# Two RWKV head pairs in step, on 64x64 products, in a hybrid mLSTM and RWKV-7 layer

## The chip, the cores and the metric

One core of a Trainium2 chip runs the whole layer for one sequence of 2048 tokens, width 1024. The metric is the time of one execution on the device in microseconds (us). TensorE's clock has two levels, 1.2 and 2.4 GHz; the profile gives the granted clock as a share of the higher one.

## The reference, cut to what matters

The layer normalises its input, projects it (`u @ w_in`), and feeds two groups of heads. Four mLSTM heads of 128 use a convolution, a gated matrix memory and an output gate. Eight RWKV-7 heads of 64 use a recurrence over tokens:

```python
def step(S, inp):
    r_t, w_t, k_t, v_t, a_t, b_t = inp
    sa = jnp.einsum('bhij,bhj->bhi', S, a_t)
    S = S * w_t[:, :, None, :] + sa[..., None] * b_t[:, :, None, :] + v_t[..., None] * k_t[:, :, None, :]
    return S, jnp.einsum('bhij,bhj->bhi', S, r_t)
```

`S` is a 64x64 state per head. The outputs of a head are normalised over its 64 values (mean and variance), scaled, given a bonus `sum(r*k*r_k)*v`, and gated. An output projection, cross-attention into 256 memory tokens, and a SwiGLU feed-forward part follow; the change touches none of these.

## The kernel before, in words

The first stage (`pre_pass`) normalises and transposes the input into f16 high and low halves, kept in device memory as `u_d`. The mixer then makes four passes (`mixer_pass`, `hp`), one for each pair of RWKV heads (128 columns: a head on each 64 partitions) and one mLSTM head. A pass loads and splits its own weights (`wraw`, L262 to L266, then `split`, L48 and L49), then goes through eight blocks of 256 tokens. Large products (`mm3`, L53 to L55) are three f16 products each, high times high, high times low, low times high.

RWKV is computed in chunks of 64 tokens, four to a block. `prepare` makes, for a block, the three projections `kps`, `rps`, `vps`, the decays, and the operands AR (read side) and KB (write side). It turns `v` (L368) and KB (L391) by TensorE's transpose, and multiplies KB by AR (`aps`, L379), where each head uses its own 64 rows but 128 columns of weights. The products are masked (L383 to L386) into M, RR and AY. `solve` inverts the triangular matrices of two blocks together, on GpSimd in 31 steps (L420, L422) with trips through device memory. `scan` carries the state through the four chunks: R from L458, times the inverse (L467), and the new state from L472, with the old state and the values stacked on all 128 rows: a head's state stands on its own 64 rows and its values on the other head's. ScalarE copies each result out of PSUM (L460, L470), VectorE decays and adds (L464, L476). When the last chunk is through, the outputs `yps` (L482, L485) are computed. A `tail` normalises them, later.

Blocks go in groups of two: prepare both, solve both, scan them one after the other, then the mLSTM part of both. The `u` pool holds eight tiles of each half, that is two blocks. A planner orders the instructions on each engine before the run, from its own estimate of their times; each engine then executes its queue in that order. In the last pass the mLSTM parts of the last four blocks are put behind everything else.

Of the kernel before, what the change touches and what calls it, by code (L numbers as in the profile page):

```python
# [105 lines left out]
def rwkv_consts(c, pool, I):  # L106
# [10 lines left out]
    c.ind = pool.tile([P, 2], F32, name="ind")  # L117
    nc.vector.memset(c.ind, 0.0)
    nc.vector.memset(c.ind[0:64, 0:1], 1.0)
    nc.vector.memset(c.ind[64:128, 1:2], 1.0)  # L120
# [124 lines left out]
def mixer_pass(c, I, hp, tp, T):  # L245
# [3 lines left out]
    GS = min(2, T // SGN)  # L249
    w_in = I["w_in"][0]  # L250
    ct = hp
    cs = slice(ct * P, (ct + 1) * P)
# [3 lines left out]
    cols = [Q0 + ct * P, Q0 + 512 + ct * P, Q0 + 1024 + ct * P, ct * P, 512 + ct * P, 1024 + ct * P, 1536 + ct * P]  # L256
    wts = [], []
    for n, o in ((3, Q0), (4, 0)):
        for k in range(KT):
            wk = w_in[k * P:(k + 1) * P, :]  # L260
            raw = tp.x.tile([P, n * P], F32, tag=f"wraw{n}", name="wraw", bufs=4 if n == 3 else 2)
            nc.sync.dma_start(raw.rearrange("p (j c) -> p j c", j=n),  # L262
                              wk[:, o:o + 512 * n].rearrange("p (j c) -> p j c", j=n)[:, :, cs])
            h = tp.w.tile([P, n * P], F16, tag=f"wh{n}", name="wh", bufs=12 if n == 3 else 9)
            l = tp.w.tile([P, n * P], F16, tag=f"wl{n}", name="wl", bufs=12 if n == 3 else 9)
            split(nc, h, l, raw, c.gmix[:, k:k + 1])  # L266
            wts[n - 3].append((h, l))

    carry = tp.k.tile([P, 3], F32, tag="carry", name="carry")
    nc.gpsimd.memset(carry, 0.0)  # L270
    Sc = tp.k.tile([P, 64], F32, tag="Sc", name="Sc")
    nc.gpsimd.memset(Sc, 0.0)
    halo = tp.k.tile([P, 2, 3], F32, tag="halo", name="halo")
    nc.gpsimd.memset(halo, 0.0)
    st = Ctx()
    st.Cn = tp.m2.tile([P, P + 1], F32, tag="Cn", name="Cn")
    nc.gpsimd.memset(st.Cn, 0.0)

    def project(ps, j, u):
        for k in range(KT):  # L280
            h, l = wts[j > 2][k]
            o = (j - 3 if j > 2 else j) * P
            s = slice(o, o + P)
            mm3(nc, ps, (h[:, s], l[:, s]), u[k], k == 0, k == KT - 1)

    def shifted(ps, j, o):
        t = tp.t2.tile([P, SGN + 1], F32, tag="tmu", name="tmu")
        m = 4 * j + ct
        nc.gpsimd.tensor_copy(t[:, 0:1], carry[:, j:j + 1])
        nc.scalar.activation(t[:, 1:SGN + 1], ps, AF.Copy, scale=c.mu_s[:, m:m + 1])  # L290
        nc.gpsimd.tensor_copy(carry[:, j:j + 1], t[:, SGN:SGN + 1])
        nc.vector.scalar_tensor_tensor(o, ps, c.mu_c[:, m:m + 1], t[:, 0:SGN], op0=ALU.mult, op1=ALU.add)  # L292
        return o

    def prepare(sg, u, M):
        g = Ctx()
        t0 = sg * SGN
        xwa = [tp.t2.tile([P, SGN], F16, tag=f"xwa{i}", name="xwa") for i in range(2)]
        for i in range(2):
            nc.sync.dma_start(xwa[i], c.l_d[0][i][:, t0:t0 + SGN])  # L300
        sl = tp.sl
        AR = tp.t1.tile([P, 4, P], F32, tag="AR", name="AR")
        g.RR = next(tp.RR)
        g.M = M
        g.AY = sl.tile([P, 4, 2, 64], F32, tag="AY", name="AY")
        g.KBt = sl.tile([P, 4, 2, 64], F32, tag="KBt", name="KBt")
        g.VS = sl.tile([P, 4, 2, 64], F32, tag="VS", name="VS")
        g.VX = sl.tile([P, 4, 2, 64], F32, tag="VX", name="VX")
        g.bon = sl.tile([P, SGN], F32, tag="bon", name="bon")
        g.W = sl.tile([P, 4, 1], F32, tag="W", name="W")  # L310
        KB = tp.t1.tile([P, 4, 192], F32, tag="KB", name="KB")
# [19 lines left out]
        nc.gpsimd.tensor_copy(g.W, E[:, :, 64:65])  # L331

        ps = tp.pmm.tile([P, SGN], F32, tag="mm", name="kps")
        project(ps, 1, u)
        k = shifted(ps, 1, tp.t2.tile([P, SGN], F32, tag="k", name="k"))
        ps = tp.pmm.tile([P, SGN], F32, tag="mm", name="rps")
        project(ps, 0, u)
        r = shifted(ps, 0, tp.t2.tile([P, SGN], F32, tag="r", name="r"))
        ps = tp.pmm.tile([P, SGN], F32, tag="mm", name="vps")
        project(ps, 2, u)  # L340
        v = shifted(ps, 2, tp.t2.tile([P, SGN], F32, tag="v", name="v"))
# [18 lines left out]
        nc.scalar.copy(KB[:, :, 128:192], KB[:, :, 0:64])  # L360
# [4 lines left out]
        nc.vector.tensor_tensor(g.bon, bps, v, ALU.mult)  # L365
        vps = tp.pax.tile([P, 2, P], F32, tag="ax", name="vps")
        for m in range(2):
            nc.tensor.transpose(vps[:, m], v[:, m * P:(m + 1) * P], c.ident)  # L368
        for h in range(2):
            for e in range(2):  # L370
                nc.scalar.copy(g.VS[halves[1 - h], e::2, h], vps[halves[e], :, 64 * h:64 * h + 64])
        for h in range(2):
            nc.gpsimd.tensor_copy(g.VX[halves[1 - h], :, h], g.VS[halves[1 - h], :, h])
        kcs = [slice(64 * (1 - h), 64 * (1 - h) + P) for h in range(2)]
        axs = [tp.pax.tile([P, 4, P], F32, tag="ax", name="aps") for _ in range(2)]
        for n in range(4):
            for h in range(2):
                b = halves[h]
                nc.tensor.matmul(axs[h][:, n], lhsT=KB[b, n, kcs[h]], rhs=AR[b, n], start=True, stop=True)  # L379
        for h in range(2):  # L380
            b, ob, aps = halves[h], halves[1 - h], axs[h]
            bc = lambda r, cc: c.mask[r, cc].unsqueeze(1).to_broadcast([r.stop - r.start, 4, 64])
            nc.vector.tensor_tensor(g.M[b], aps[b, :, 0:64], bc(b, b0), ALU.mult)  # L383
            nc.vector.tensor_tensor(g.RR[ob, :, h, 0:64], aps[ob, :, 0:64], bc(ob, b0), ALU.mult)
            nc.scalar.copy(g.RR[b, :, h], AR[b])
            nc.vector.tensor_tensor(g.AY[:, :, h], aps[:, :, 64:128], bc(slice(0, P), b1), ALU.mult)  # L386
        kps = [tp.pax.tile([P, 4, 64], F32, tag="ax", name="kbps") for _ in range(2)]
        for n in range(4):
            for h in range(2):
                b = halves[h]  # L390
                nc.tensor.transpose(kps[h][:, n], KB[b, n, kcs[h]], c.ident[b, b])  # L391
        for h in range(2):
            nc.scalar.copy(g.KBt[:, :, h], kps[h])
        return g

    def solve(MX, NG):
# [3 lines left out]
        MXu = MX.rearrange("p g u t -> p (g u) t")  # L400
# [49 lines left out]
    def scan(sg, g, g2, fresh):  # L450
        y = tp.s2.tile([P, 2, 2, 64], F32, tag="y", name="y")
        if fresh:
            for h in range(2):
                nc.scalar.copy(g.VS[halves[h], 0, h], Sc[halves[h]])
        for n in range(4):
            ch = tp.psc.tile([P, 3, 64], F32, tag="ch", name="ch")
            for h in range(2):
                nc.tensor.matmul(ch[halves[h], 0], lhsT=g.RR[:, n, h, 0:64], rhs=g.VS[:, n, h], start=True, stop=True)  # L458
            R = tp.s2.tile([P, 64], F32, tag="R", name="R")
            nc.scalar.copy(R, ch[:, 0])  # L460
            Sw = tp.s2.tile([P, 64], F32, tag="Sw", name="Sw")
            for h in range(2):
                b = halves[h]
                nc.vector.tensor_scalar(Sw[b], g.VS[b, n, h], g.W[b, n], None, op0=ALU.mult)  # L464
            for h in range(2):
                b = halves[h]
                nc.tensor.matmul(ch[b, 1], lhsT=g.M[b, n], rhs=R[b], start=True, stop=True)  # L467
            for h in range(2):
                b = halves[h]
                nc.scalar.copy(g.VX[b, n, h], ch[b, 1])  # L470
            for h in range(2):
                last = nc.tensor.matmul(ch[halves[h], 2], lhsT=g.KBt[:, n, h], rhs=g.VX[:, n, h], start=True, stop=True)  # L472
            for h in range(2):
                b = halves[h]
                dst = g.VS[b, n + 1, h] if n < 3 else g2.VS[b, 0, h] if g2 is not None else Sc[b]
                nc.vector.scalar_tensor_tensor(dst, ch[b, 2], g.W[b, n], Sw[b], op0=ALU.mult, op1=ALU.add)  # L476
        yps = tp.psc.tile([P, 2, 2, 64], F32, tag="Y", name="yps")
        with tc.issue_after(last.ins):
            for m in range(2):
                for h in range(2):  # L480
                    for n in (2 * m, 2 * m + 1):
                        nc.tensor.matmul(yps[halves[n % 2], m, h], lhsT=g.RR[:, n, h, 64:128], rhs=g.VS[:, n, h],  # L482
                                         start=True, stop=False)
                    for n in (2 * m, 2 * m + 1):
                        nc.tensor.matmul(yps[halves[n % 2], m, h], lhsT=g.AY[:, n, h], rhs=g.VX[:, n, h],  # L485
                                         start=False, stop=True)
        nc.vector.tensor_copy(y, yps)

        def tail():
            y4 = y.rearrange("p m h i -> p (m h) i")  # L490
            mean = tp.s2.tile([P, 4], F32, tag="mean", name="mean")
# [930 lines left out]
```

## Time and profile before

| what | us |
|---|---|
| median of three runs | 3099.39 |
| the runs | 3096.95, 3099.39, 3101.4 |
| profiled execution | 3100.74 |
| its span, first to last instruction | 3099.0 |

A matmul's time in the trace runs from its start to the modelled end of its result, so matmuls overlap: how fast they follow one another is read from their starts. PE is TensorE's products, PEld its weight loads, DVE is VectorE, ACT is ScalarE, POOL is GpSimd. A shape such as 64*64 64x64 f32 gives the rows and columns of the array that the weights take, then the shape of what streams through. An entry in brackets behind a row tells how long the engine was idle before it and what ended that. The page puts the feed-forward part and the attention behind the mixer; the profile rows that follow are of the mixer and of its start.

### The profile page before, as it was taken

The numbers are of one execution on the slowest core, as the hardware profiler recorded it, in microseconds if no ns is written. First come the engines' busy times: TensorE is split into PE (matmuls) and PEld (weight loads), VectorE is DVE, ScalarE is ACT, GpSimd is POOL, SyncE is SP. The second block draws the span as 40 slices with busy tenths as digits, with TensorE's granted clock in tenths as the row PEclk, the third lists the DMA queues.
The fourth block names the chain that finished last, engine by engine and source line by source line (L and its number), as shares of the span: only waits on it lengthen the run. The fifth ranks groups of instructions, "written<-read, shape, count | busy, mean of one in ns | idle before, by whom it ended". The sixth has DMA issues, their size and how long they took to land. (4 is left out here: it accounts for less than half of the span.)

```text
span 3099.0 us, 55710 instructions
## 1 busy us (share of the span) xinstructions
PE 2956.4 (95%) x20515; PEld 1776.2 (57%) x20515; DVE 2155.9 (70%) x4150; ACT 1299.8 (42%) x3098; POOL 1199.7 (39%) x2189
## 2 busy tenths in 40 slices
PE   7799999999999988999999999999999999899998
PEld 4577777778777767646555554444444444344443
DVE  6568877787687867627788887554454555897975
ACT  6445544554455445506656654222222222423332
POOL 2156654555555665003412134222222221644642
PEclk9899999999999988999999999999999999999999
DMA  8522422232232223555323357122111111554442
GB/s 278 130 76 63 105 70 68 76 97 75 63 80 64 77 70 99 183 167 171 124 76 108 107 194 242 58 67 67 55 55 55 55 58 58 184 185 145 151 144 75
DMA packets 393966, 331.01 MB, mean 107 GB/s; under 512 B 92654, under 2 KB 343772, under 8 KB 392796
## 3 DMA queue, kind: packets, MB, share of 16 engines
q1 hardware_dynamic: 393692, 327.45, 34.5%
q8 instruction: 161, 2.64, 0.3%
q14 instruction: 113, 0.93, 0.1%
HBM read 231.86 MB, written 95.49 MB: 106 GB/s over the span
## 5 line engine op out<-in xcount | busy, mean ns | idle before, releaser
L53 PE MATMUL pp<-u,wb 128*128 128x512 f16 x1232 | 467.5, 379 | 13.5 <-DVE e L1127 10.1
L54 PE MATMUL pp<-u,wb 128*128 128x512 f16 x1232 | 467.7, 380 | 0.0
L55 PE MATMUL pp<-u,wb 128*128 128x512 f16 x1232 | 467.3, 380 | 0.0
L1127 DVE TENSOR_TENSOR e<-pp,e 128x512 f32<-128x512 f32 x308 | 208.5, 689 | 301.6 <-PE pp L55 288.1
L55 PE MATMUL dps<-w,gS 128*128 128x512 f16 x616 | 234.6, 381 | 7.5 <-DVE gS L49 7.5
L54 PE MATMUL dps<-w,gS 128*128 128x512 f16 x616 | 234.7, 381 | 1.7 <-DVE w L49 1.7
L53 PE MATMUL dps<-w,gS 128*128 128x512 f16 x616 | 234.8, 381 | 0.0
L420 POOL TENSOR_TENSOR tmp<-M,X 64x126 f32<-64x126 f32 (+22 forms) x496 | 194.9, 393 | 74.2 <-DMA M<-md 45.9
L422 POOL TENSOR_TENSOR X<-X,tmp 64x126 f32<-64x126 f32 (+22 forms) x496 | 204.3, 412 | 30.1
L54 PEld LDWEIGHTS <-wb 128*128 128x128 f16 x1232 | 120.6, 98 | 157.1 <-issue 13.4
L53 PEld LDWEIGHTS <-wb 128*128 128x128 f16 x1232 | 120.7, 98 | 149.5 <-DMA u<-u_d 3.9
L55 PEld LDWEIGHTS <-wb 128*128 128x128 f16 x1232 | 120.7, 98 | 146.0 <-issue 0.6
L1143 POOL TENSOR_TENSOR S<-raw 128x512 f32<-128x512 f32 x22 | 33.3, 1515 | 411.2 <-DVE wb L49 411.2
L54 PEld LDWEIGHTS <-wh 128*128 128x128 f16 x1280 | 128.0, 100 | 36.0 <-issue 16.1
L53 PE MATMUL qps<-uh,wh 128*128 128x256 f16 x512 | 140.8, 275 | 2.0 <-DVE r L292 1.1
L53 PEld LDWEIGHTS <-wh 128*128 128x128 f16 x1280 | 128.4, 100 | 24.3 <-issue 2.2
L55 PEld LDWEIGHTS <-wl 128*128 128x128 f16 x1280 | 128.3, 100 | 22.5 <-issue 1.9
L53 PE MATMUL vops<-wh,uh 128*128 128x256 f16 x512 | 139.9, 273 | 1.1 <-ACT cv L539 0.8
L55 PE MATMUL qps<-uh,wl 128*128 128x256 f16 x512 | 140.6, 275 | 0.0
L54 PE MATMUL qps<-ul,wh 128*128 128x256 f16 x512 | 140.5, 274 | 0.0
L55 PE MATMUL vops<-wh,ul 128*128 128x256 f16 x512 | 139.8, 273 | 0.0
L54 PE MATMUL vops<-wl,uh 128*128 128x256 f16 x512 | 139.7, 273 | 0.0
(428 smaller groups left out, 7895.2 us busy)
## 6 DMA issues: line engine op xcount, KB each, us to landing
g_d<-e SPq DMA_DIRECT2D x88, 256.0 KB
uh<-u_d SPq DMA_DIRECT2D x144, 128.0 KB
ul<-u_d SPq DMA_DIRECT2D x144, 128.0 KB
h<-h_d SPq DMA_DIRECT2D x32, 512.0 KB
acc<-h_d SPq DMA_DIRECT2D x32, 512.0 KB
u_d<-ub SPq DMA_DIRECT2D x56, 256.0 KB
ga<-g_d SPq DMA_DIRECT2D x32, 384.0 KB
raw<-in_ffn_w_gate_dram SPq DMA_DIRECT2D x22, 512.0 KB
```

The costliest lines, as they stand in the source:

```text
L53: nc.tensor.matmul(out, lhsT=lhs[0], rhs=rhs[0], start=start, stop=False)
L54: nc.tensor.matmul(out, lhsT=lhs[0], rhs=rhs[1], start=False, stop=False)
L55: nc.tensor.matmul(out, lhsT=lhs[1], rhs=rhs[0], start=False, stop=stop)
L420: nc.gpsimd.tensor_tensor(tv, M[:, s, s + 1:32].unsqueeze(2).to_broadcast(shp), X[:, s, 0:ncl].unsqueeze(1).to_broadcast(shp), ALU.mult)
L422: nc.gpsimd.tensor_tensor(X[:, s + 1:32, 0:ncl], X[:, s + 1:32, 0:ncl], tv, ALU.add)
L1127: add = lambda o, x, y: nc.vector.tensor_tensor(o, x, y, ALU.add)
L1143: nc.gpsimd.tensor_tensor(s[0], a[1][0], a[1][1], ALU.add)
```

## The change

Two passes (`hq`) take the place of four. A pass loads the weights of two head pairs and two mLSTM heads, in eight tiles of each kind (raw tiles: two and one buffers, before four and two). A group is now one block with both pairs (`e` is 0 or 1): prepare both, solve both together, scan both in step, then the two mLSTM parts.

All small RWKV products now use a head's own 64 rows and its own 64 columns. The values V and what was VX (now X) are no longer stacked with the other head's state; each of the chain's and of the outputs' products gets one part for each operand. Transposes of v, KB and y become products with the identity (`turn`); v's uses `cent`, the identity minus 1/64, so that the values have zero mean over a head and the tail's mean is not computed. The state's decay is applied in one instruction for both pairs, after an addition for both. The bonus keeps the values as they were.

```diff
-            raw = tp.x.tile([P, n * P], F32, tag=f"wraw{n}", name="wraw", bufs=4 if n == 3 else 2)
-            h = tp.w.tile([P, n * P], F16, tag=f"wh{n}", name="wh", bufs=12 if n == 3 else 9)
+            raw = tp.x.tile([P, n * 2 * P], F32, tag=f"wraw{n}", name="wraw", bufs=2 if n == 3 else 1)
+            h = tp.w.tile([P, n * 2 * P], F16, tag=f"wh{n}", name="wh", bufs=8)
...
+    c.cent = pool.tile([P, 64], F32, name="cent")
+    for b in (0, 64):
+        nc.vector.tensor_scalar(c.cent[b:b + 64], c.ident[b:b + 64, b:b + 64], -1.0 / 64, None, op0=ALU.add)
...
+    def turn(out, x, by):
+        nc.tensor.matmul(out, lhsT=x, rhs=by, start=True, stop=True)
...
-            nc.tensor.transpose(vps[:, m], v[:, m * P:(m + 1) * P], c.ident)
+                turn(vps[halves[h], n], v[halves[h], n * 64:n * 64 + 64], c.cent[halves[h]])
+        nc.scalar.copy(G.V[:, e], vps)
+        for o, dst in ((64, g.M), (0, g.KY)):
+            aps = tp.pax.tile([P, 4, P], F32, tag="ax", name="aps")
+            for n in range(4):
+                for h in range(2):
+                    b = halves[h]
+                    nc.tensor.matmul(aps[b, n], lhsT=KB[b, n, o:o + 64], rhs=AR[b, n], start=True, stop=True)
+            nc.vector.tensor_tensor(dst, aps, c.mask.unsqueeze(1).to_broadcast([P, 4, P]), ALU.mult)
...
+                    turn(kps[halves[h], n, i], KB[halves[h], n, 64 * i:64 * i + 64], c.ident[halves[h], halves[h]])
...
+        def both(out, *parts):
+            for i, (l, r) in enumerate(parts):
+                for b in halves:
+                    last = nc.tensor.matmul(out[b], lhsT=l[b], rhs=r[b], start=i == 0, stop=i == len(parts) - 1)
+            return last
         for n in range(4):
+            S = state(n)
+            ch = tp.psc.tile([P, 2, 3, 64], F32, tag="ch", name="ch")
+            for e, g in enumerate(gs):
+                both(ch[:, e, 0], (g.AR[:, n, 0:64], S[:, e]), (g.KY[:, n, 0:64], G.V[:, e, n]))
+            R = tp.s2.tile([P, 2, 64], F32, tag="R", name="R")
+            nc.scalar.copy(R, ch[:, :, 0])
+            for e, g in enumerate(gs):
+                both(ch[:, e, 1], (g.M[:, n, 0:64], R[:, e]))
+            nc.scalar.copy(G.X[:, :, n], ch[:, :, 1])
+            for e, g in enumerate(gs):
+                last = both(ch[:, e, 2], (g.KBt[:, n, 1], G.X[:, e, n]), (g.KBt[:, n, 0], G.V[:, e, n]))
+            Sn = tp.s2.tile([P, 2, 64], F32, tag="Sn", name="Sn")
+            nc.vector.tensor_tensor(Sn, ch[:, :, 2], S, ALU.add)
...
+            nc.vector.tensor_tensor(dst, Sn, G.W[:, :, n].to_broadcast([P, 2, 64]), ALU.mult)
...
+                    both(yps[:, e, n], (g.AR[:, n, 64:128], state(n)[:, e]), (g.M[:, n, 64:128], G.X[:, e, n]),
+                         (g.KY[:, n, 64:128], G.V[:, e, n]))
...
+                        turn(tps[b, e, n * 64:n * 64 + 64], y[b, e, n], c.ident[b, b])
...
+    for sg in range(NS):
+        u = load_u(sg)
+        G = group(sg)
+        gs = [prepare(sg, e, u, G) for e in range(2)]
+        solve(G.MX, 2)
+        stails.append(scan(sg, gs, G))
```

## Rows read from the trace of the kernel before

**Rows 1.** The page, part 1: engine, busy us (share of the span) xinstructions.

```profile
PE 2956.4 (95%) x20515; PEld 1776.2 (57%) x20515; DVE 2155.9 (70%) x4150; ACT 1299.8 (42%) x3098; POOL 1199.7 (39%) x2189
```

**Rows 2.** Windows view: start:end, length, engines' busy time, clock, DMA share, GB/s.

```profile
130.00:1215.00 1085.00, 1021.18 (x10297) 812.10 (x10298) 818.17 (x2110) 533.45 (x1631) 596.14 (x1599) 0.96 0.29 75
```

**Rows 3.** Timeline of TensorE, one chain burst: start, us, line, shape, count.

```profile
686.56 0.27 PE L55 MATMUL qps<-uh,wl 128*128 128x256 f16 x1
686.67 0.27 PE L53 MATMUL qps<-uh,wh 128*128 128x256 f16 x1
686.87 0.33 PE L467 MATMUL ch<-R,MX 64*64 64x64 f32 x4
687.14 0.28 PE L54 MATMUL qps<-ul,wh 128*128 128x256 f16 x1
```

**Rows 4.** The timeline of TensorE in an output burst (yps).

```profile
733.24 0.34 PE L472 MATMUL ch<-VX,KBt 128*64 128x64 f32 x4
733.41 0.29 PE L482 MATMUL yps<-VS,RR 128*64 128x64 f32 x4
733.52 0.29 PE L485 MATMUL yps<-VX,AY 128*64 128x64 f32 x4
733.64 0.29 PE L482 MATMUL yps<-VS,RR 128*64 128x64 f32 x4
```

**Rows 5.** Lines view, TensorE, shapes apart: count, busy us, mean ns, idle before.

```profile
L458 PE MATMUL ch<-VS,RR 128*64 128x64 f32 x512 | 47.4, 254 | 13.6 <-DVE VS L476 9.3 <-DVE Sc L476 2.9 <-ACT VS L454 1.0
L391 PE MATMUL kbps<-ident,KB 64*128 64x64 f32 x256 | 28.6, 244 | 1.4 <-DVE AY L386 0.9 <-ACT KBt L393 0.2
```

**Rows 6.** The timeline of TensorE around one aps burst.

```profile
631.87 0.27 PE L53 MATMUL kps<-uh,wh 128*128 128x256 f16 x1
632.08 1.16 PE L379 MATMUL aps<-AR,KB 64*128 64x128 f32 x8
633.16 0.28 PE L54 MATMUL kps<-ul,wh 128*128 128x256 f16 x1
```

**Rows 7.** The timeline of TensorE around kbps and vps transposes.

```profile
690.48 0.38 PE L368 MATMUL vps<-ident,v 128*128 128x128 f32 x2
690.70 0.27 PE L55 MATMUL qps<-uh,wl 128*128 128x256 f16 x1
...
747.41 0.27 PE L55 MATMUL gps<-xg,lg 128*128 128x256 f16 x1
747.61 0.46 PE L391 MATMUL kbps<-ident,KB 64*128 64x64 f32 x4
748.00 0.49 PE L564 MATMUL skp<-qk 128*128 128x128 f32 x2
```

**Rows 8.** Source view of line L467: duration ns min/median/max, first and last start.

```profile
L467 PE MATMUL ch<-R,MX x512: 218/267/366, 215.3 to 1384.5; 64*64 64x64 f32 x171
```

**Rows 9.** The lines view of VectorE and ScalarE, 100 to 1390 us.

```profile
L464 DVE TENSOR_SCALAR Sw<-VS,W 64x64 f32<-64x64 f32 x256 | 75.9, 297 | 14.1 <-ACT VS L454 8.4
L476 DVE SCALAR_TENSOR_TENSOR VS<-ch,W,Sw 64x64 f32<-64x64 f32 x224 | 62.5, 279 | 53.3 <-PE ch L472 33.9 <-issue 12.6 <-ACT KBt L393 1.3
L383 DVE TENSOR_TENSOR MX<-aps,mask 64x256 f32<-64x256 f32 x64 | 26.9, 420 | 22.2 <-PE aps L379 21.4
L713 DVE SCALAR_TENSOR_TENSOR xt<-ops,xt 128x512 f32<-128x512 f32 x16 | 10.9, 691 | 46.7 <-PE ops L55 34.1 <-DMA xt<-in_x_dram 12.6
L470 ACT COPY VX<-ch 64x64 f32<-64x64 f32 x256 | 52.5, 205 | 77.2 <-PE ch L467 75.3
```

**Rows 10.** The windows view before the first projections, and the weights' DMA issues.

```profile
80.00:90.00 10.00, 6.02 (x45) 3.74 (x43) 5.08 (x10) 4.73 (x9) 0.00 (x0) 1.00 0.95 279
...
wraw<-in_w_in_dram SPq DMA_DIRECT2D x32, 256.0 KB
wraw<-in_w_in_dram SPq DMA_DIRECT2D x32, 192.0 KB
```

**Rows 11.** The windows view of five stretches, and the timeline inside the first.

```profile
500.00:520.00 20.00, 15.33 (x118) 10.42 (x116) 14.08 (x33) 6.94 (x21) 13.87 (x38) 0.67 0.07 21
560.00:590.00 30.00, 26.51 (x293) 19.48 (x293) 19.81 (x55) 14.01 (x44) 11.88 (x34) 0.83 0.14 37
780.00:800.00 20.00, 16.32 (x159) 11.26 (x157) 16.86 (x43) 8.69 (x27) 8.69 (x31) 0.92 0.17 44
840.00:870.00 30.00, 27.11 (x266) 21.13 (x263) 17.82 (x54) 13.11 (x40) 9.66 (x28) 0.77 0.18 48
1090.00:1140.00 50.00, 37.42 (x434) 27.30 (x436) 32.60 (x80) 20.86 (x62) 23.95 (x66) 0.81 0.22 54
...
514.98 0.37 PE L53 MATMUL vps<-uh,wh 128*128 128x256 f16 x1 [1.84 <-DVE k L292]
515.14 0.42 PE L54 MATMUL vps<-ul,wh 128*128 128x256 f16 x1
```

More of the change, by code (lines that the diff above doesn't have):

```diff
@@ L280, in project, with shifted @@
+    st.Cn = []
+    for e in range(2):
+        st.Cn.append(tp.m2.tile([P, P + 1], F32, tag=f"Cn{e}", name="Cn"))
+        nc.gpsimd.memset(st.Cn[e], 0.0)
+    def project(ps, j, e, u):
         for k in range(KT):
             h, l = wts[j > 2][k]
-            o = (j - 3 if j > 2 else j) * P
+            o = (2 * (j - 3 if j > 2 else j) + e) * P
             s = slice(o, o + P)
             mm3(nc, ps, (h[:, s], l[:, s]), u[k], k == 0, k == KT - 1)
-    def shifted(ps, j, o):
+    def shifted(ps, j, e, o):
@@ new lines, in group @@
+    def group(sg):
+        G = Ctx()
+        G.xwa = [tp.t2.tile([P, SGN], F16, tag=f"xwa{i}", name="xwa") for i in range(2)]
+        for i in range(2):
+            nc.sync.dma_start(G.xwa[i], c.l_d[0][i][:, sg * SGN:(sg + 1) * SGN])
+        G.MX = tp.MX.tile([P, 2, 4, P], F32, tag="MX", name="MX")
+        G.V = tp.sg.tile([P, 2, 4, 64], F32, tag="V", name="V")
+        G.X = tp.sg.tile([P, 2, 4, 64], F32, tag="X", name="X")
+        G.S = tp.sg.tile([P, 2, 3, 64], F32, tag="S", name="S")
+        G.bon = tp.sg.tile([P, 2, SGN], F32, tag="bon", name="bon")
+        G.W = tp.sg.tile([P, 2, 4, 1], F32, tag="W", name="W")
+        return G
@@ L312, in prepare @@
+    def prepare(sg, e, u, G):
+        g = Ctx()
+        ct = 2 * hq + e
+        cs = slice(ct * P, (ct + 1) * P)
+        xwa, sl = G.xwa, tp.sl
+        AR = g.AR = sl.tile([P, 4, P], F32, tag="AR", name="AR")
+        g.M = G.MX[:, e]
+        g.KY = sl.tile([P, 4, P], F32, tag="KY", name="KY")
+        g.KBt = sl.tile([P, 4, 2, 64], F32, tag="KBt", name="KBt")
+        KB = tp.t1.tile([P, 4, P], F32, tag="KB", name="KB")
         v4 = "p (n t) -> p n t"
@@ L374, in prepare @@
-        kcs = [slice(64 * (1 - h), 64 * (1 - h) + P) for h in range(2)]
-        axs = [tp.pax.tile([P, 4, P], F32, tag="ax", name="aps") for _ in range(2)]
+        nc.vector.tensor_tensor(G.bon[:, e], bps, v, ALU.mult)
+        vps = tp.pax.tile([P, 4, 64], F32, tag="ax", name="vps")
         for n in range(4):
             for h in range(2):
[L378 to L386, printed above, removed]
@@ L394, in prepare @@
+        kps = tp.pax.tile([P, 4, 2, 64], F32, tag="ax", name="kbps")
+        for n in range(4):
+            for i in range(2):
+                for h in range(2):
+                    turn(kps[halves[h], n, i], KB[halves[h], n, 64 * i:64 * i + 64], c.ident[halves[h], halves[h]])
+        nc.scalar.copy(g.KBt, kps)
         return g
@@ L448, in solve @@
             nc.scalar.copy(MXu[a, :, 32:64], xps[a])
[L450 to L454, printed above, removed]
-        for n in range(4):
[L456 to L477, printed above, removed]
-        with tc.issue_after(last.ins):
[L479 to L486, printed above, removed]
@@ L501, in tail @@
-            nc.gpsimd.tensor_tensor(y4, y4, var.unsqueeze(2).to_broadcast([P, 4, 64]), ALU.mult)
-            tps = tp.psx.tile([P, SGN], F32, tag="sx", name="tps")
-            for m in range(2):
-                nc.tensor.transpose(tps[:, m * P:(m + 1) * P], y[:, m].rearrange("p h i -> p (h i)"), c.ident)
-            yc = tp.s2.tile([P, SGN], F32, tag="dq", name="yc", bufs=1)
-            nc.scalar.activation(yc, tps, AF.Identity, bias=col(c, R_LNB + ct), scale=col(c, R_LNW + ct))
-            xg = [tp.s2.tile([P, SGN], F16, tag=f"xg{i}", name="xg") for i in range(2)]
+            nc.gpsimd.tensor_tensor(var, var, c.mhalf.unsqueeze(2).to_broadcast([P, 2, 4]), ALU.pow)
@@ new lines, in tail @@
+            nc.gpsimd.tensor_tensor(y, y, var.unsqueeze(3).to_broadcast([P, 2, 4, 64]), ALU.mult)
+            tps = tp.psx.tile([P, 2, SGN], F32, tag="sx", name="tps")
+            for e in range(2):
+                for n in range(4):
+                    for b in halves:
+                        turn(tps[b, e, n * 64:n * 64 + 64], y[b, e, n], c.ident[b, b])
+            yc = tp.s2.tile([P, 2, SGN], F32, tag="dq", name="yc", bufs=1)
+            for e in range(2):
+                ct = 2 * hq + e
+                nc.scalar.activation(yc[:, e], tps[:, e], AF.Identity, bias=col(c, R_LNB + ct), scale=col(c, R_LNW + ct))
@@ L508, in tail @@
+            xg = [tp.s2.tile([P, SGN], F16, tag=f"xg{i}", name="xg", bufs=1) for i in range(2)]
             for i in range(2):
                 nc.sync.dma_start(xg[i], c.l_d[1][i][:, sg * SGN:(sg + 1) * SGN])
-            gps = tp.psx.tile([P, SGN], F32, tag="sx", name="gps")
-            mm3(nc, gps, (c.lg[0][:, cs], c.lg[1][:, cs]), xg, True, True)
-            nc.vector.tensor_tensor(yc, yc, g.bon, ALU.add)
+            gps = tp.psx.tile([P, 2, SGN], F32, tag="sx", name="gps")
+            for e in range(2):
+                cs = slice((2 * hq + e) * P, (2 * hq + e + 1) * P)
+                mm3(nc, gps[:, e], (c.lg[0][:, cs], c.lg[1][:, cs]), xg, True, True)
```

179 lines of the change are left out of this document (63 added, 116 removed).

## The prediction

> **What bounds the kernel now.** I read the page's first part, then the RWKV/mLSTM stage by a window, then single bursts in order of time, and last the products by line and shape for their counts. The page has TensorE busy in 95% of the span [rows 1], so the question is what the stage that the change touches pays for. In its middle, 130 to 1215 us, TensorE is busy 1021 of 1085 us at a granted clock of 0.96 of full speed, VectorE 818 us, ScalarE 533 us, GpSimd 596 us [rows 2]. Busy time at full clock is 1021.18 x 0.96 = 980 us; 105 us are idle or lost to the lower level of 1.2 GHz. TensorE is thus the engine that bounds the stage, and 105 us is all that faster helpers could ever give back there. But a busy TensorE is not a useful one: in [rows 3] consecutive 256-column f16 products start 0.11 us apart, while a burst of four chain instructions set between them moves the next f16 start from 0.11 to 0.47 us later (686.67 to 687.14). The burst costs 0.36 us. How much of it is streaming is seen where bursts run on: in [rows 4] four such instructions start 0.115 us after the four before (733.41, 733.52, 733.64), that is 0.029 each, or 0.058 for a pair of instructions on the two halves of the array's columns (I call such a pair a slot). So 0.36 = 2 x 0.058 + 0.24, and 0.24 us is the price of going from the full array to the small shape and back.
>
> **The change part by part.** The unit is one 256-token block with two pairs of heads; there are 16 of them either way, and eight blocks times four head pairs before are eight blocks times two double pairs after. The rows count two instructions for each f32 product and one for a transpose [rows 5].
>
> 1. *Chain.* Before, each 64-token step has three bursts of four instructions per head pair: 4 steps x 3 x 2 pairs = 24 bursts of 0.36 = 8.6 us. After, both pairs share a burst, 12 in all; but the state and value parts, once stacked on 128 rows, are two products on 64 rows, so bursts have 8, 4 and 8 slots: 4 x (0.70 + 0.47 + 0.70) = 7.5 us. Gain 1.1 x 16 = 18 us.
> 2. *Outputs (yps).* 64 instructions (2 x 32) become 96, three parts instead of two: 32 x 0.029 = 0.93 us more, x 16 = +15 us.
> 3. *aps.* 32 instructions of 128 columns, 8 to a burst that costs 633.16 - 631.87 - 0.11 = 1.18 us [rows 6]: they do not overlap, (1.18 - 0.24)/8 = 0.12 each. After, 64 instructions in 32 slots of 128 columns; twice the 64-column slot is 0.116. Cost 0.
> 4. *kbps.* Eight transposes per pair in two bursts of four; one burst costs 748.00 - 747.41 - 0.11 = 0.48 us [rows 7], so 1.92 a block. After: per pair 32 instructions, 16 slots, in one burst 0.24 + 0.93 = 1.17; 2.34 a block. +0.42 x 16 = +7 us.
> 5. *vps.* Two full-array transposes per pair, 0.22 us with no switch (690.48 to 690.70) [rows 7], become 8 slots in a burst of their own, 0.70: +0.97 a block, +15 us.
> 6. *tps.* The same four transposes a block (0.44) become 16 slots and a burst, 1.17: +0.73, +12 us.
>
> TensorE sum: -18 + 15 + 0 + 7 + 15 + 12 = **+31 us**. The projections and the mLSTM products keep number and shape: 0. No row shows more than two slots of a 64x64 shape in succession, so the 0.058 is taken from the 128x64 rows. Bounds: four L467 instructions last 0.33 us [rows 3] and one of them 0.218 at the shortest [rows 8], so the second slot starts about 0.107 after the first; if every slot took that, the 192 slots of 64 columns in a block (80 chain, 48, 32, 16, 16) x 0.049 x 16 = +150 us on top; below, if the new vps and kbps bursts run on into others of their shape, 64 switches of 0.24 are saved, -15 us. I take 0.058, as the one row of the 64x64 shape [rows 3] has the same length for four instructions, 0.33 us, as the 128x64 one (0.34) [rows 4].
>
> A rule speaks against step 1 to 6: the Trainium skill (TensorEngine Tiling (Array Packing), "Gotcha 1: PSUM Pressure") has it that tiles on different rows cannot write the same PSUM bank at once, and after the change nearly all pairs do. The trace disagrees so far: L467 writes both halves of one ch tile from different rows in 0.33 us. It stays as a rival below.
>
> 7. *VectorE* loses L464 and L476, 76 + 62 us (L476's last step of a group apart), and gets two 128x128 instructions a double step; between L476's 64x64 row (0.279) and a 128x512 row (0.691) I put these at 0.33: 128 x 0.33 = 42 [rows 9]. The masks, three such rows of 64 at 0.42 (one shown), 80 us, become 64 at 0.69: 44. So some 130 us go, a sixth of the 818, and the dropped mean and merged tails add to it. All of it lies off TensorE's path except where TensorE waits.
> 8. *ScalarE* loses in the same way (L470's 256 copies, 52 us, become 64 larger ones), GpSimd its value copies. Neither bounds: 0, as cover.
> 9. *Weights.* Before, a pass reads 8 x (192 + 256) KB, now twice that, in two passes instead of four. Just before the first projections DMA is at 0.95 of its engines and 279 GB/s [rows 10]. The RWKV half must be there before the first projection: 1.57 MB more / 279 GB/s = **+6 us**; bounds 0 (hidden behind the end of the first stage) and +12 (both halves queued ahead). The reload between passes now has eight buffers for eight tiles; up to +15 us if no product is left to hide it, against two boundaries fewer: 0.
> 10. *Waits.* Five stretches, 150 us long, show span minus busy x clock of 9.7, 8.0, 5.0, 9.1 and 19.7 = 52 us [rows 11], half of the 105 in a seventh of the time. There TensorE has chain and preparation only and waits for helpers: at 514.98 a projection sat 1.84 us until VectorE's shifted k was out, and ran at 1.2 GHz afterwards (0.42 instead of 0.27) [rows 11]. With 130 us less on VectorE, half as many serial chain steps, and the u buffers (eight of each kind) holding two blocks, which are now two groups instead of one, there is more to put there. I take **-52 us**: the five stretches or as much elsewhere. Bounds 0 and -79 (three quarters of 105). What is late next is TensorE's own streaming.
>
> Sum: 3100.7 (the profiled execution, span 3099.0) + 31 + 6 - 52 = 3086; that execution lay 1.3 above the median of the three runs, so **3084 us**.
>
> **The rivals.**
> A, the forecast: 3084, own range 3055 to 3112.
> B, slower: TensorE stays the bound and the waits come back. The order of work is fixed before the run; waits come wherever it guessed a helper's time wrongly, and longer chain bursts (0.70 instead of 0.36) delay the f16 stream just as much. For it: of the 64 us idle in [rows 2] no single helper has much. Against it: the low-clock stretches start at a VectorE wait. Price: nothing given back, 3100.7 + 37 = 3138, 3136 at the median, with a bad reload 3151. It decides as soon as less than 37 us of waiting goes.
> C, larger gain: 79 us of waits go, the small bursts join (-15), the start is hidden: 3100.7 + 16 - 79 = 3038, 3036 at the median. For it: the doubled reach of the u buffers and the loss of a sixth of VectorE's work; against it: it leaves 26 us of waits in 1085.
> D, the pairs do not overlap: 192 slots x 0.049 x 16 = 150 us, and the 32 aps slots a further 0.107 each, 55: 3289. That is also the time by the rule cited above. Against it the L467 row.
>
> **How the numbers follow.** A 0.42, B 0.33, C 0.20, D 0.05. The range goes from C to B with its bad reload, 3030 to 3155; D and what little lies outside is left out. What this kernel's runs can tell from no change is about 0.2%, 6 us: faster means below 3093. A is below that in two cases of three and within 0.2% in one of six, C always, B almost never: faster 0.42 x 0.66 + 0.20 + 0.01 = 0.49; same 0.42 x 0.16 + 0.33 x 0.06 = 0.09; slower 0.42.
>
> **What would show it.** Steps 1 to 6: a chain burst of 16 instructions between f16 products should take 0.70, and rows on the 64x64 shape should start 0.115 apart per four; 0.2 would be D. Step 7: VectorE's busy time in the stage down by 130 us or more. Step 10: the same formula over the stage should leave about 53 us instead of 105, with fewer stretches at a lower clock. The forecast is wrong if TensorE's waiting in the stage stays above 70 us, or if switching is cheaper or dearer than 0.24 for the larger bursts.

## The result, and the profile after

The changed kernel takes 3176.16 us in the median of four runs (3173.41 to 3180.99) against 3098.17 for the kernel before (3096.19 to 3101.4): 1.0252 times as long, 95% interval 1.0235 to 1.027. The profiled execution took 3173.77 us, with a span of 3172.0. The prediction, 3084 with a range to 3155, was wrong in its sign.

The page's first part, to set beside [rows 1]: VectorE, ScalarE and GpSimd all work less, TensorE 40 us more.

```profile
PE 2996.7 (94%) x24227; PEld 1853.2 (58%) x24227; DVE 1958.1 (62%) x3413; ACT 1158.0 (37%) x2522; POOL 1152.2 (36%) x2077
```

The windows view of the changed kernel, with the columns of [rows 2]: first the stretch of those rows, then the whole mixer, from the first projection to the first product of the output projection (`ops`).

```profile
130.00:1215.00 1085.00, 998.01 (x13109) 829.17 (x13107) 597.36 (x1364) 372.75 (x1027) 516.97 (x1407) 0.95 0.21 51
97.00:1379.00 1282.00, 1164.94 (x15080) 969.02 (x15078) 709.25 (x1634) 461.85 (x1253) 579.65 (x1566) 0.94 0.23 59
```

The mixer of the kernel before in the same view:

```profile
97.00:1294.00 1197.00, 1116.29 (x11215) 887.45 (x11212) 891.28 (x2311) 596.44 (x1790) 619.33 (x1670) 0.95 0.32 83
```

The mixer starts at the same time in both and becomes 85 us longer; what follows it is 12 shorter (3172 - 1379 against 3099 - 1294). Of the 85, TensorE's busy time is 49 (1164.94 - 1116.29) and its idle time 36 (117.1 against 80.7). Busy time times the granted clock rises from 1060 to 1095; each is good to 6 us, since the clock has two digits. So at full clock TensorE's own work grew by about 35 us, and idle time with the time lost to the low clock by about 50. VectorE, meanwhile, lost 182 us of work and GpSimd 40: the relief came and brought no time back.

What TensorE does inside a burst came as worked out. The timeline of the changed kernel, first R and then M of the chain, to set beside [rows 3]:

```profile
506.16 0.27 PE L55 MATMUL qps<-uh,wl 128*128 128x256 f16 x1
506.36 0.33 PE L454 MATMUL ch<-S,AR 64*64 64x64 f32 x4
506.52 0.28 PE L454 MATMUL ch<-V,KY 64*64 64x64 f32 x4
506.64 0.28 PE L454 MATMUL ch<-S,AR 64*64 64x64 f32 x4
506.76 0.28 PE L454 MATMUL ch<-V,KY 64*64 64x64 f32 x4
506.97 0.50 PE L324 MATMUL wps<-xwa,lwa 64*128 64x256 f16 x6
...
509.71 0.27 PE L53 MATMUL qps<-uh,wh 128*128 128x256 f16 x1
509.91 0.45 PE L454 MATMUL ch<-R,MX 64*64 64x64 f32 x8
510.29 0.28 PE L54 MATMUL qps<-ul,wh 128*128 128x256 f16 x1
```

Rows of four start 0.12 us apart (0.16 after the first), 0.03 an instruction, the burst of eight costs 510.29 - 509.71 - 0.11 = 0.47 and that of sixteen 506.97 - 506.16 - 0.11 = 0.70, to the digit what steps 1 to 6 put them at. (The row behind the sixteen is itself a 64-row product; the 38 bursts of sixteen in this trace that stand between two full-array f16 products without a wait, at full clock, cost 0.707 in the median.) All of it lands in one `ch` tile from both row halves. That settles the rule cited against the change (the Trainium skill, TensorEngine Tiling (Array Packing), "Gotcha 1: PSUM Pressure"): in this trace such pairs do overlap, four instructions in 0.12 us.

Where TensorE stands still in the changed kernel, by the waits view (engine, operation, line, what it waited for: us in all, times, longest):

```profile
PE pps L436 <- DMA T<-t1d: 27.2, 14, 4.5
PE kps L53 <- DVE r L290: 13.8, 7, 4.2
PE kbps L294 <- DVE MX L383: 10.1, 1, 10.1
PE ymps L599 <- ACT nsb L579: 7.6, 3, 5.8
PE ncp L574 <- DVE kt L567: 6.6, 2, 3.9
```

The first lines of the same view of the kernel before:

```profile
PE aps L379 <- ACT VS L371: 11.4, 5, 7.2
PE ch L472 <- ACT VX L470: 11.1, 21, 1.1
PE vps L53 <- DVE k L292: 10.9, 5, 5.3
PE ch L458 <- DVE VS L476: 9.3, 8, 2.3
```

The chain's own waits (L472, L458) are no longer among the largest, which is what step 10 was after. In their place stands the return of the solve: `pps`, the first product with the inverse, waits 27.2 us for the transfer that GpSimd's steps end in. In the kernel before, TensorE came to `pps` 32 us after GpSimd's last step (median of the 16 solves in its trace); now it does so after 5 us (4.9 to 6.2 in all 16), mostly the moment the transfer is through.

### The profile page after: what moved, and what is told of

Read it like the earlier page. It is cut to its first block, busy times and chain, and to the rows that moved or that the text cites. A ratio compares the mean times of both kernels' runs of the same rounds, so it can differ in the third digit from the quotient of the medians.

```text
span 3172.0 us, 61123 instructions
## 1 busy us (share of the span) xinstructions
PE 2996.7 (94%) x24227; PEld 1853.2 (58%) x24227; DVE 1958.1 (62%) x3413; ACT 1158.0 (37%) x2522; POOL 1152.2 (36%) x2077
## 5 line engine op out<-in xcount | busy, mean ns | idle before, releaser
L416 POOL TENSOR_TENSOR tmp<-M,X 64x126 f32<-64x126 f32 (+22 forms) x496 | 187.2, 377 | 143.6 <-DMA M<-md 115.1
L1126 POOL TENSOR_TENSOR S<-raw 128x512 f32<-128x512 f32 x22 | 33.8, 1536 | 410.5 <-DVE wb L49 410.5
```

Source lines behind the costliest of these rows:

```text
L416: nc.gpsimd.tensor_tensor(tv, M[:, s, s + 1:32].unsqueeze(2).to_broadcast(shp), X[:, s, 0:ncl].unsqueeze(1).to_broadcast(shp), ALU.mult)
L1126: nc.gpsimd.tensor_tensor(s[0], a[1][0], a[1][1], ALU.add)
```

## The experiments

The changed kernel lies 78 us over the kernel before (3176.16 - 3098.17). Of each run the distance to the kernel before on its own chip is taken (3100.2 for e1 to e4, 3101.7 for e5 to e8, 3100.3 for e9 to e11, 3101.5 for e12 to e15, 3104.7 for e16 to e18). "Over the changed kernel" is that distance less 78. Busy and idle are TensorE's in the mixer, read as above. The 95% intervals of the ratios are 0.2 to 0.4% wide, so differences between two runs of under some 8 us are not clear of noise.

### The two halves of the change: e1 and e2

**e1_shape_only** keeps four passes and groups of two blocks, with the small products in the new shapes:

```diff
-                nc.tensor.matmul(ch[halves[h], 0], lhsT=g.RR[:, n, h, 0:64], rhs=g.VS[:, n, h], start=True, stop=True)
+            both(ch[:, 0], (g.AR[:, n, 0:64], S), (g.KY[:, n, 0:64], g.V[:, n]))
```

> Four passes, groups of two blocks and the step order of the kernel before; only the small RWKV products have the changed kernel's shapes (own 64 rows and columns, turns by products, values centred). Theory (T): the change lost through two things, about +40 us of TensorE work from the shapes, net of the bursts that stepping saves, and about +35 us of waits from the new grouping. Then this kernel, which doubles the slots of each burst and saves no burst, pays 28 (chain) + 15 (yps) + 7 (kbps) + 15 (vps) + 15 (tps) = 80 us of TensorE work, with the waits of before: 3160 to 3180 us. Rival R (the grouping, the weights and the pass change are all of it): 3090 to 3115 us.

3142.18 us (3139.58 to 3143.12), ratio 1.0129 (1.0114 to 1.0144), 42 us slower: between the two expectations.

**e2_step_only** keeps the old shapes, layouts and tail, and puts two pairs in step in two passes. To make room, seven mLSTM tiles have one buffer instead of two.

```diff
-        for hp in range(4):
+        for hq in range(2):
...
+            ch = tp.psc.tile([P, 2, 3, 64], F32, tag="ch", name="ch")
+                    nc.tensor.matmul(ch[halves[h], e, 0], lhsT=g.RR[:, n, h, 0:64], rhs=G.VS[:, e, n, h], start=True, stop=True)
```

> Two passes and both pairs in step as in the changed kernel, but the products keep the shapes of before (state and values stacked on 128 rows, transposes, mean in the tail); seven mLSTM tiles have one buffer instead of two, to make room. Theory T: chain bursts are halved (12 of 0.47 us instead of 24 of 0.36 a block: -48 us) and the grouping costs about +35 us of waits: 3075 to 3100 us. Rival R (grouping is all of the loss): 3130 to 3180 us. Rival S (the shapes are all of it, grouping costs nothing): 3045 to 3060 us.

3084.71 us (3078.13 to 3089.56), ratio 0.9947 (0.9929 to 0.9965): 15.5 us faster, theory T's range, though not by T's terms, as the table shows. **It beats both kernels.** The mixer's row in e1's windows view:

```profile
95.00:1338.00 1243.00, 1162.24 (x14847) 951.73 (x14845) 738.10 (x1858) 488.59 (x1420) 587.03 (x1598) 0.97 0.31 80
```

and in e2's:

```profile
95.00:1284.00 1189.00, 1085.37 (x11303) 881.87 (x11301) 803.37 (x1927) 563.04 (x1568) 620.92 (x1637) 0.96 0.26 64
```

| | busy | idle | clock | busy x clock against before | the rest of the mixer against before | mixer against before |
|---|---|---|---|---|---|---|
| before | 1116 | 81 | 0.95 | | | |
| shapes alone (e1) | 1162 | 81 | 0.97 | +67 | -21 | +46 |
| step alone (e2) | 1085 | 104 | 0.96 | -18 | +10 | -8 |
| both | 1165 | 117 | 0.94 | +35 | +50 | +85 |

Busy time times clock is TensorE's work at full clock, good to some 6 us a row; the rest of the mixer is idle time and what the low clock took. The shapes cost TensorE 67 us of work, the step saves 18. (T had put these at 80 and 48, and the waits of the step at 35, so its range for e2 came true by two errors that cancel.) Added up, the mixer should be 38 longer; both together gave +85. The 47 over are not work: with both, the work is 14 less than the sum of the halves, while the rest is +50 where -11 would be due. In e1 the rest even fell by 21, with VectorE relieved in much the same way (891 to 738 us), through a higher clock at the same idle time: there, with passes and groups as before, a part of what step 10 hoped for came. With the step alone come 23 us of idle time, and the solve's return, under 3 us in the kernel before, is a part of them, as e2's waits show:

```profile
PE pps L447 <- DMA T<-t1d: 14.0, 15, 2.4
```

The rest of the runs ask where the 47 come from.

### Is it the solve's return, or the order around it: e3, e5, e6, e8

**e3_early** issues the next block's preparation and solve ahead of the scan, mLSTM part and tail of the block before:

```diff
-        stails.append(scan(sg, gs, G))
+        if ahead is not None:
+            rest(*ahead)
+        ahead = sg, u, G, gs
```

> The changed kernel with another order: a block's projections, products and triangular solve are issued ahead of the scan, the mLSTM part and the tail of the block before it, so that these stand beside the solve's trip through GpSimd and device memory. Same instructions. Theory T: the 27 us that TensorE waits at pps for the solve and some of the waits behind it go, 25 to 45 us: 3130 to 3150 us. Rival S (TensorE's work is the loss, order does not matter): 3170 to 3182 us.

3185.71 us (3180.83 to 3192.88), ratio 1.0272 (1.0251 to 1.0294): 8 us over the changed kernel. T is out.

**e5_short_after** and **e6_short_before** run every second step of the solve:

```diff
-        for s in range(31):
+        for s in range(0, 31, 2):
```

> The changed kernel with every second of GpSimd's 31 solve steps left out (the outputs are then wrong), so a solve takes about 16 us less and nothing on TensorE, VectorE or ScalarE changes. Theory W (in the new form TensorE has too little to do between the end of a block's preparation and the return of its solve, and that loop sets the pace): the 27 us before the first sum of the solve (pps) and some of the waiting that follows go, 3130 to 3148 us, and the pps wait falls under 8 us. Rival L (TensorE's own longer streaming and many short waits, the solve is hidden): 3165 to 3178, and what waits at pps turns up elsewhere.

> Control: the kernel before with the same half of the solve's steps left out. Theory W says that the old form hides the solve (2.3 us of waiting at its return in the whole stage): 3090 to 3102 us. If it gains as much as the changed kernel does (over 20 us), the solve was exposed in both forms and W explains nothing of the difference.

3171.73 us (1.0222, 1.0208 to 1.0236) and 3110.91 (1.0029, 1.0019 to 1.0039): 8 us less in the new form, 9 more in the old, although GpSimd's work in the mixer fell from 580 to 399 and from 619 to 431 us. W is out. The wait it was to remove is still there in e5, beside one that has grown from 7.6 us, as e5's waits show:

```profile
PE ymps L599 <- ACT nsb L579: 35.2, 6, 7.6
PE pps L436 <- DMA T<-t1d: 23.0, 13, 6.8
```

The planner put the consumer of the shorter solve earlier, and TensorE waited there again: from the first step of a solve to its `pps`, TensorE has 222 full-array products in the changed kernel and 116 in e5 (medians of 16), GpSimd's steps take 33.0 and 15.5 us, and `pps` follows the last step by 5 us in both. So the largest line of a list of waits need not be a limit: it can be where the plan was a little too early.

**e8_step_z2** is e2 with `z` doubled again and `mb` single.

```diff
-            z = m2.tile([P, SGN + 3], F32, tag="z", name="z", bufs=1)
+            z = m2.tile([P, SGN + 3], F32, tag="z", name="z")
```

> The two-pass form on the old shapes again, with the convolution's input tile (z) doubled as it was before and the mLSTM's mb row single to make room. Theory T (its waits, 21.7 us before the mLSTM value projection and 12 us before the next q/k projections, came from the single z): 3058 to 3074 us. Rival R (they are the form's own, and move to another wait): 3080 to 3088, with the sum of the listed waits unchanged.

3092.05 us (0.9962, 0.995 to 0.9975): its distance to before is 6 us smaller than e2's, which the intervals leave open. T is out: the wait for the mLSTM value projection fell from 21.7 to 13.2 us, that for the solve rose from 14.0 to 19.3, and no time was gained.

### What an added product costs: e4 and e7

**e4_turns_twice** does every `turn` twice; **e7_outputs_twice** does the three parts of each output twice.

```diff
+        for _ in range(2):
             nc.tensor.matmul(out, lhsT=x, rhs=by, start=True, stop=True)
...
-                    both(yps[:, e, n], (g.AR[:, n, 64:128], state(n)[:, e]), (g.M[:, n, 64:128], G.X[:, e, n]),
+                    both(yps[:, e, n], *2 * ((g.AR[:, n, 64:128], state(n)[:, e]), (g.M[:, n, 64:128], G.X[:, e, n]),
```

> The changed kernel with every turn (values, KB, outputs) done twice in place: 64 more slots a block of 0.058 us, no more bursts, 64 x 0.058 x 16 = 59 us. If TensorE's stream sets the pace throughout (both S and T for the shape part): 3225 to 3240 us. If the pace is set by waits into which slots fit: 3176 to 3205 us.

> The changed kernel with the three parts of each output product done twice (96 more TensorE instructions a block, 16 blocks, on a 64x64 shape, in bursts that are there already; nothing waits for them but the tail, and the outputs are wrong). Theory P (a small product costs its 0.029 us per instruction where no loop passes through it, and the double of it only where it delays the solve, as when the turns were doubled): 96 x 16 x 0.029 = 45 us, 3213 to 3232. Rival Q (any added TensorE work in this form costs about twice its streaming, wherever it stands): 3255 to 3275.

3296.48 (1.0628, 1.061 to 1.0646) and 3283.12 us (1.0576, 1.0558 to 1.0594): 118 and 103 over the changed kernel, about twice what they stream. Both of e4's ranges were far too low and Q's a little: added products cost this also where no loop passes through them. The extra is not in the products, as the first and the last row of such a burst show, in the changed kernel and in e7:

```profile
460.38 0.33 PE L454 MATMUL ch<-X,KBt 64*64 64x64 f32 x4
464.05 0.28 PE L454 MATMUL ch<-V,KY 64*64 64x64 f32 x4
...
977.84 0.33 PE L454 MATMUL ch<-X,KBt 64*64 64x64 f32 x4
984.30 0.28 PE L454 MATMUL ch<-V,KY 64*64 64x64 f32 x4
```

The burst has 128 instructions in the first case and 224 in the second, and the 96 more take 6.46 - 3.67 = 2.79 us: 0.029 each, 45 us for 16 blocks. The mixer of e7 has 35 us more busy and 79 more idle time than the changed kernel:

```profile
96.00:1492.00 1396.00, 1200.27 (x16619) 1012.47 (x16616) 701.36 (x1633) 463.69 (x1252) 570.86 (x1567) 0.92 0.22 55
```

Its waits have moved to `ncp`, a product of the mLSTM part, which the change does not touch:

```profile
PE ncp L574 <- DVE kt L567: 55.3, 9, 10.8
PE pps L436 <- DMA T<-t1d: 27.5, 14, 10.3
PE skp L561 <- DVE ym L49: 25.8, 2, 14.0
```

A wait of 9 us at `ncp` in e7's timeline (in brackets: idle before, and what ended it):

```profile
575.78 0.27 PE L54 MATMUL rps<-ul,wh 128*128 128x256 f16 x1
...
582.56 0.39 POOL L418 TENSOR_TENSOR X<-X,tmp 64x110 f32<-64x110 f32 x1
582.91 0.70 POOL L592 TENSOR_TENSOR ss<-ss,mhalf 128x2 f32<-128x2 f32 x1
...
583.65 0.33 DVE L593 SCALAR_TENSOR_TENSOR r<-r,ss 128x2 f32<-128x2 f32 x1 [11.38 <-POOL ss L592]
...
584.36 0.41 DVE L565 TENSOR_TENSOR Em<-Em,skp 128x256 f32<-128x256 f32 x1
584.69 0.42 DVE L567 TENSOR_TENSOR kt<-skp,tk 128x256 f32<-128x256 f32 x1
...
585.25 0.77 PE L574 MATMUL ncp<-vx,Em 128*128 128x129 f32 x2 [9.20 <-POOL tmp L416]
...
586.67 0.42 PE L55 MATMUL rps<-uh,wl 128*128 128x256 f16 x1
```

TensorE's `ncp` products read `Em` and `kt`; VectorE has both queued behind `r`; `r` needs a root of 128x2 values, which GpSimd has queued between steps of a solve. (The bracket of `ncp` names such a step, because it ended last, at 585.12; `kt` ended at 585.11.) Each engine keeps its planned order; nine microseconds pass while TensorE's next products, the rest of `rps`, which has been under way since before, stand behind `ncp`. Afterwards they run at the lower clock (0.42 instead of 0.27).

### Is it that one instruction: e12 to e15

VectorE's wait for this root (L595 in the kernel before, L592 in the others) is 19.4 us in the kernel before, 65.2 in the changed one, 123.6 in e7. e12, e13 and e14 take it out of the changed kernel, the kernel before and e7:

```diff
-            nc.gpsimd.tensor_tensor(ss, ss, c.mhalf.to_broadcast([P, 2]), ALU.pow)
```

> The changed kernel without one 128x2 GpSimd instruction in the mLSTM tail (the inverse square root of the mLSTM normalisation; the outputs lack it). VectorE's next instruction there waits for it, 19 us in the kernel before, 65 in the changed kernel, 124 with doubled outputs, because it stands in GpSimd's queue between steps of the next solve; all of VectorE's queue stands behind that wait. Theory V (this is the place where TensorE's gain is lost): 3110 to 3140 us. Rival U (any helper's queue does it; with this wait gone the order finds another): 3155 to 3178.

> Control: the kernel before without the same instruction. Theory V: its wait is short here, 3083 to 3098 us, so that the difference to the changed kernel falls from 75 to 45 us or less, which is about TensorE's own added work. Rival U: 3090 to 3105, difference still 65 to 80.

> The changed kernel with doubled output products (45 us of streaming, which cost 107) and without that instruction. Theory V: 40 to 60 us over e12. Rival U: 80 us or more over e12.

3183.68 (1.0263), 3095.72 (0.9981, 0.9972 to 0.999) and 3278.56 us (1.0567). V is out: the changed kernel comes out 4 us slower (not clear of noise, and above U's range too), the old one 6 faster, and the difference is 88 instead of 78; the doubled outputs still cost 95. Another wait takes its place, as U said; in e12:

```profile
PE kps L53 <- DVE r L290: 42.3, 12, 6.0
PE pps L436 <- DMA T<-t1d: 22.6, 13, 4.3
```

**e15_step_own_root** is e2 with the root made on VectorE, from a first guess in integers and three of these steps:

```diff
+                nc.vector.tensor_tensor(t, y, y, ALU.mult)
+                nc.vector.scalar_tensor_tensor(t, t, -0.5, ss, op0=ALU.mult, op1=ALU.mult)
+                nc.vector.scalar_tensor_tensor(y, t, 1.5, y, op0=ALU.add, op1=ALU.mult)
```

> The two-pass form on the old shapes (e2, 3085 us) with the same inverse square root computed on VectorE itself by eleven small instructions instead of GpSimd's one; the outputs are the reference's. Theory V: 3060 to 3078 us, as 28 us of VectorE's waiting go. Rival U: 3080 to 3092.

3092.02 us (0.9968, 0.9955 to 0.998), 6 nearer to before than e2, again within the intervals; U at its upper end, and V is out here too.

### Is it the order: e9 to e11

The same instructions, ordered by the planner's other estimate of times:

```diff
-    with tile.TileContext(nc, schedule_with_timeline_sim=True) as tc:
+    with tile.TileContext(nc, schedule_with_timeline_sim=False) as tc:
```

> The kernel before, its instructions unchanged, ordered by the planner's other way of estimating times; only the order of the queues differs. Baseline for the next two: any time from 3100 to 3250 us. By itself it tells how much the order alone is worth.

> The changed kernel ordered in the same other way. Theory G (the extra waiting of the changed kernel comes from where the order puts the consumers, since the order is made beforehand from a guess of times that is off for the new small products): against e9 the difference is that of TensorE's work alone, plus 30 to 50 us, or it even changes its sign, instead of plus 75. Rival H (the waiting comes from what depends on what in the new form, whatever the order): plus 70 to 90 us against e9.

> The changed kernel with its output products done twice, ordered in the other way. They stream for 45 us; in the usual order they cost 107. Theory G: the cost depends on the order, 35 to 60 us against e10. Rival H: again about 100 us or more.

3449.34 (1.1122), 3405.7 (1.0987) and 3444.15 us (1.1111). This order costs the kernel before 349 us, far more than expected. In it the **change makes the kernel 44 us faster**, and the doubled outputs cost 38, less than they stream. G, with its sign changed; H is out. The mixer in e9, e10 and e11:

```profile
104.00:1625.00 1521.00, 1183.91 (x11369) 903.64 (x11370) 898.82 (x2369) 619.76 (x1826) 621.67 (x1675) 0.88 0.27 67
```

```profile
99.00:1582.00 1483.00, 1175.15 (x15109) 967.46 (x15106) 722.91 (x1639) 480.78 (x1257) 565.13 (x1566) 0.89 0.21 54
```

```profile
100.00:1624.00 1524.00, 1227.83 (x16633) 1017.27 (x16631) 723.99 (x1639) 477.77 (x1256) 563.85 (x1566) 0.89 0.21 52
```

From e9 to e10 idle time falls from 337 to 308; from e10 to e11 busy time rises by 53 and idle time falls by 12. Here TensorE waits so much that there is time to give back, and some comes, as step 10 of the prediction took for granted in the tuned order. It also means that this order has slack to hide a cost in, so the test is weaker for e11 than for the sign.

### Which work, in which form: e16 to e18

e16 does the output products of the kernel before three times; e17 and e18 put three full-array f32 products ahead of the output products of the changed kernel and the kernel before. The first two lines are e16's, the last two e17's:

```diff
+                    for i in range(3):
+                            nc.tensor.matmul(yps[halves[n % 2], m, h], lhsT=g.RR[:, n, h, 64:128], rhs=g.VS[:, n, h],
...
+                for _ in range(3):
+                    nc.tensor.matmul(yps[:, e], lhsT=c.ident, rhs=G.X[:, e], start=True, stop=True)
```

> The kernel before with its output products done three times: 128 more small instructions a block at 0.029 us, 16 blocks, 59 us of streaming. Theory G (the order is made from a guess of times in which pairs of small products on the two halves of the array do not overlap, so that work put beside them is found unfinished): they cost about twice that, 100 to 140 us, in the old form too: 3200 to 3240. Rival X (the new form is tighter, any work added to it costs double, and the old form takes it at its price): 50 to 70, 3150 to 3170.

> The changed kernel with three full-array f32 products of 128x256 put ahead of each pair's output products (their result is overwritten): 6 a block, two instructions each of about 0.21 us, 16 blocks: 41 us of streaming, in the place where the doubled outputs cost 107 for 45. Theory G: work of a full-array shape is guessed rightly and costs its streaming, 30 to 55 us, 3205 to 3230. Rival X: 80 to 110 us, 3255 to 3285.

> The kernel before with the same three full-array products ahead of each block's output products: again 41 us of streaming. Both theories: 30 to 55 us, 3130 to 3155; if it is 80 or more, the old form is as tight as the new one and both are wrong about what differs.

3161.15 us (1.0183, 1.0168 to 1.0198), 3211.27 (1.0346, 1.0329 to 1.0363) and 3136.76 (1.0097, 1.0073 to 1.012).

| added, in the usual order | stream | time | busy | idle |
|---|---|---|---|---|
| 64x64 pairs in the new form (e7) | 45 | +103 | +35 | +79 |
| 64x64 turns in the new form (e4) | 59 | +118 | +62 | +60 |
| full-array products in the new form (e17) | 41 | +29 | +38 | -8 |
| 128x64 pairs in the old form (e16) | 59 | +56 | +54 | +6 |
| full-array products in the old form (e18) | 41 | +32 | +43 | -7 |

X fits e16 and is out with e17: the new form takes full-array products at their price. G, as it was put (any pair of small products is misjudged, in both forms), is out as well: 128x64 pairs cost what they stream. What costs double is the 64x64 pair in the changed kernel and in the usual order; in the other order it does not. That is what a plan would do that prices this shape wrongly, so that the work put beside it is not done when TensorE comes to it. But three things speak for caution. e1 has the same shapes in nearly all its small products, in the usual order, and pays for them no more than TensorE's own work. e7 adds 1536 instructions and e17 only 192, so that in the new form the shape and the number are not told apart. And VectorE's wait for the outputs (`y`) grows wherever something is put ahead of them, by 62 us in e7 (from 3.5), but also by 32 in e17, 33 in e16, 24 in e18 and 37 in e11, which pay no more than the streaming. The planner's price itself was not read, and neither 64x64 pairs in the old form nor 128x64 pairs in the new one were multiplied: the reading is a guess that the table allows, not one that it shows. What is shown is that the time hangs on the order.

## Why the prediction was wrong, step by step

1. *Steps 1 to 6, TensorE: +31.* Right in sum; the single terms were not measured. The slot of 0.058 and the 0.47 for an M burst stand in the rows above, and rival D is out. The mixer's busy time rose by 49, and by 35 when weighed with the clock; the forecast was made at full clock, so the 35 is what it has to be compared with, and the rest of the 49 is a lower clock.
2. *Steps 7 and 8, the helpers' relief.* Larger than said on VectorE: 818 to 597 us in the stage [rows 2], but that stretch now holds less of the mixer; over the whole mixer 891 to 709, so 182 instead of some 130 and what the dropped mean was to add. Its rows came near: two 128x128 instructions a double step at 0.285 and 0.288 (0.33 forecast), the masks at 0.689 (0.69).

```profile
L383 DVE TENSOR_TENSOR MX<-aps,mask 128x512 f32<-128x512 f32 x32 | 22.1, 689 | 42.8 <-PE aps L382 42.1 <-DMA ul<-u_d 0.6
...
L475 DVE TENSOR_TENSOR S<-Sn,W 128x128 f32<-128x128 f32 x48 | 13.8, 288 | 0.5
L470 DVE TENSOR_TENSOR Sn<-ch,S 128x128 f32<-128x128 f32 x48 | 13.7, 285 | 20.5 <-PE ch L454 19.2 <-issue 1.1
```

3. *Step 9, the start: +6.* It cost nothing, its lower bound: the first projection starts at 97 us in both.
4. *Step 10, the waits: -52 ("I take -52 us", bounds 0 and -79).* **This is the step that failed.** By its own formula the stage lost 105 us before and loses 1085 - 998.01 x 0.95 = 137 now, where 53 were forecast and 70 was the sign of being wrong; over the whole mixer the same formula gives +50, of which 36 are idle time. Against -52 that is a miss of some 100 us, more than the whole miss of 92; the start and what follows the mixer gave a little back. The step read the waits as a debt of the helpers, to be paid by making them faster. e5 and e12 took away the work behind a large wait, e8 the shortage of a buffer behind one, and the waits stayed or moved on while the time stayed within 8 us; e9 to e11 kept the work and changed the order, and the sign of the change turned. So in the tuned order the waits follow the plan; that they are what is left where plan and chip differ is a reading, not a measurement. The bounds had no room above nothing, though nearly all small products were about to get a shape that the queues before hold in one line only (L467).
5. *The rivals.* B named the mechanism ("waits come wherever it guessed a helper's time wrongly") and its point of decision was met, but its price stopped at waits that stay; they grew, so 3176 lies above its 3151. C is out.

What stays open is why e1, which has the same shapes, shows no growth of idle time, while both halves together lose 47 us more than their sum. That the plan has more 64x64 pairs in one place there (16 instructions to a chain burst, where e1 has 8) fits, but was not tried; nor were more buffers in the changed kernel.

## What to carry to other kernels

When TensorE is 95% busy and its queue was ordered beforehand, do not count waiting time as a reserve that faster helpers pay out: put a bound above zero on it whenever the change alters the shapes or the grouping that the order was fitted to. Before chasing the largest wait, shorten the work behind it; if the wait stays, look at the order. Split a change into its halves first: here the half that shares the bursts is worth 15 us alone, the half that reshapes the products loses 42, and the two together lose more than the sum.

## What the runs showed that was not expected

- Doubling 64x64 products in the changed kernel costs 103 for 45 us of streaming and 118 for 59, while the added output instructions themselves run at 0.029 us each.
- Halving the steps of the longest serial part (GpSimd, 580 to 399 us in the mixer) moved the time by no more than 9 us: 8 off one form, which is hardly clear of noise, and 9 more in the other.
- TensorE's consumer of the solve stood 5 us behind GpSimd's last step whether the solve took 33 us or 15.5: the plan moved it.
- The order of the queues alone, with the same instructions, is worth 349 us of 3100.
